# Packing the top-k of a 64-token chunk, a new order for gate copies, convolution products from PSUM, and ten products held behind the gate matrix

## The chip, the cores and the metric

The kernel runs on one core of a Trainium2 chip. The time is that of one execution on the device in microseconds (us); where several runs are given, their median counts.

## The reference

One layer of a hybrid decoder for 512 prompt tokens and 64 sample tokens (8 sequences of 8). Two branches, a gated short convolution and a sliding-window attention, are merged, and a layer norm gives h. Then comes the part that takes most of the time, a retrieval of experts by product keys: each token has 8 heads; a head has two queries of 128 numbers, each scored against 128 sub-keys; the best 16 of each side give pairs, and the best 16 pairs name 16 of the 16384 experts.

```python
qv = einsum('nd,de->ne', xb, w_pq).reshape(n, 8, 2, 128)
s = einsum('nhpc,hpkc->nhpk', qv, sub_keys)
top_s, top_i = lax.top_k(s, 16)
cand_s = top_s[:, :, 0, :, None] + top_s[:, :, 1, None, :]
best_s, sel = lax.top_k(cand_s.reshape(n, 8, -1), 16)      # idx: the experts that sel names
gate = softmax(best_s)
pre = einsum('nd,nhkd->nhk', xb, expert_u[idx])
out = einsum('nhk,nhkd->nd', gate * gelu(pre), expert_v[idx])
```

The convolution multiplies two projections, runs three taps over the product, and multiplies by a third projection.

## The kernel before, in words

The 576 tokens are cut into chunks of up to 128. A first window (chunks 0 and SMP, 256 rows) and a second window (chunks 1, 2 and 3, with 128, 128 and 64 rows) pass through the same stages: projections, attention, convolution (`conv_tile`, L378), merge, top-k (`scores`, L732, and `route`, L422). Every weight table comes through `table` (L136): a load of 512 KB on SP's queue, then `split` (L118) into a high part on ScalarE (L119) and a low part on GpSimd or VectorE (L120). A product (`mm3`, L122) is three matmuls for each of eight blocks, so 24 for one table.

The first window's experts are gathered row by row (`experts`, L491): an indirect load on GpSimd (L512), then a dot product or a scaled sum on VectorE (L526, L535). These steps are called from `table`, `PACE_U` of them for one table of `expert_u`, and so are spread over the rest of the program.

The second window's experts are computed densely. A front product (`front`, L833) multiplies all tokens by a table of `expert_u` (`euT`), applies a GELU on ScalarE (L840, L844) and, for the first `NS` = 60 tables, writes the result to a spill in DRAM. Gates are built as a matrix: for each of the 384 token columns, `gate_matrix` (L753) compares numbers with keys on VectorE (L766) to get two one-hots, scales one of them (L772 on ScalarE for three of four tokens, L774 on GpSimd for the fourth), multiplies them on TensorE (L775), and copies four tokens' 128x512 result to `gb` (L779 on ScalarE for three of four, L781 on VectorE for the fourth). A group of 16 tokens then goes to DRAM (L782); there are 24 groups.

The order is set as follows. `scores(second, g4)` is called for the quarters 0 to 3, with 5 front products after each. For a quarter, four products with `w_pq` give queries, these are multiplied by sub-keys into one PSUM bank a chunk (L742), a bank is copied to `sc` (L746), and `top16` (L414) runs five VectorE instructions for each of the 4 score sets of each chunk. After quarters 1 and 3, `route` runs for each chunk: top 16 of the sums, an exponential on ScalarE (L448), and two one-hot compares with the row `iota` (L470) that look up the key numbers. Then the gate groups are traced, with front products up to `AHEAD - KEEP` spread over them, and the last `KEEP` = 3 products are put behind the last gate matmul in TensorE's queue:

```python
    for i in range(len(DENSE)):
        for g in gate_matrix(i, *second.sel[i], gd):
            fronts(base + (AHEAD - KEEP - base) * (i * (128 // GN) + g + 1) // total)
    with tc.issue_after(newest[1]):
        fronts(AHEAD)
```

`AHEAD` is 69. The framework orders each engine's instructions by its own simulated times, so that engines work off in-order queues whose order is not exactly the traced one. PSUM has two banks for products with the tag `u` and three with the tag `mm`.

The last stage (L909) reads gates (L879) and spilled results (L883) back, multiplies them (L887), splits the product into `chi` and `clo`, and accumulates it with tables of `expert_v` into six PSUM banks (L917): 18 matmuls for a table. For tables past 60 a front product runs in between.

Of the kernel before, what the change touches and what calls it, by code (L numbers as in the profile page):

```python
# [60 lines left out]

ORDER = "qkscscasacsca"
FQ = 5
KEEP = 3
LAST = 2


# [8 lines left out]
def step_kernel(ctx: ExitStack, tc: tile.TileContext, I: dict, O: dict):  # L76
# [25 lines left out]
    def tmp(p, shape, tag, name=None, bufs=1, dt=F32):  # L102
        return pools[p].tile(shape, dt, tag=tag, name=name or tag, bufs=bufs)
# [274 lines left out]
    def conv_tile(ct, project, chi, clo, segs, smp):  # L378

        mv = chi.shape[2]  # L380
        npr = sum(b - a for a, b in segs)
        hs = tmp("t", [128, mv], "hs")
        y = hs
        up = tmp("t", [128, 2 + npr], "up")
        A.activation(hs, project(2), AF.Copy)
        cg = tmp("t", [128, mv], "cg")
        A.activation(cg, project(1), AF.Copy)
        V.tensor_copy(up[:, 0:2], ucar[:, ct, :])
        parts, at = [], 0
        for a, b in segs:  # L390
            V.tensor_tensor(up[:, 2 + at:2 + at + b - a], cg[:, a:b], hs[:, a:b], op=ALU.mult)
            parts.append((y[:, a:b], [up[:, at + j:at + j + b - a] for j in range(3)]))
            at += b - a
        V.tensor_copy(ucar[:, ct, :], up[:, npr:npr + 2])
        if smp:
            def tok(t):
                return t[:, smp:smp + 64].rearrange("p (b t) -> p b t", b=NB)

            us = tmp("t", [128, NB, 2 + NT], "us")
            V.tensor_copy(us[:, :, 0:2], state[:, ct])  # L400
            V.tensor_tensor(us[:, :, 2:], tok(cg), tok(hs), op=ALU.mult)
            V.tensor_copy(state[:, ct], us[:, :, NT:])
            parts.append((tok(y), [us[:, :, j:j + NT] for j in range(3)]))
        for dst, taps in parts:
            V.tensor_scalar(dst, taps[2], convw[:, ct, 2:3], None, op0=ALU.mult)
            V.scalar_tensor_tensor(dst, taps[0], convw[:, ct, 0:1], dst, op0=ALU.mult, op1=ALU.add)
            V.scalar_tensor_tensor(dst, taps[1], convw[:, ct, 1:2], dst, op0=ALU.mult, op1=ALU.add)
        bg = tmp("t", [128, mv], "bg")
        A.activation(bg, project(0), AF.Copy)
        V.tensor_tensor(y, y, bg, op=ALU.mult)  # L410
        split(chi[:, ct, :], clo[:, ct, :], y)


    def top16(val, pos, s, n):  # L414
        s2 = tmp("k", [128, 128], "s2", bufs=2)[:s.shape[0], :n]
        V.max(val[:, 0:8], s)
        V.max_index(pos[:, 0:8], val[:, 0:8], s)
        V.match_replace(s2, val[:, 0:8], s, -3.0e38)
        V.max(val[:, 8:16], s2)
        V.max_index(pos[:, 8:16], val[:, 8:16], s2)  # L420

    def route(val, pos, sel, hs):  # L422

        keys, gt = sel
        r = val.shape[0]
        val, pos = (t[:, hs * 8:hs * 8 + 8, :] for t in (val, pos))
        gt, keys = gt[:r, hs * 64:hs * 64 + 64], [t[:r, hs * 64:hs * 64 + 64] for t in keys]
        cand = tmp("k", [128, 4, NCAND], "cand")[:r]
        v4 = val.rearrange("p (h s) k -> p h s k", s=2)
        V.tensor_tensor(cand[:, :, 0:64].rearrange("p h (a b) -> p h a b", a=4),  # L430
                        v4[:, :, 0, 0:4].unsqueeze(3).broadcast_to([r, 4, 4, 16]),
                        v4[:, :, 1, :].unsqueeze(2).broadcast_to([r, 4, 4, 16]), op=ALU.add)
        V.tensor_tensor(cand[:, :, 64:112].rearrange("p h (a b) -> p h a b", a=12),
                        v4[:, :, 0, 4:16].unsqueeze(3).broadcast_to([r, 4, 12, 4]),
                        v4[:, :, 1, 0:4].unsqueeze(2).broadcast_to([r, 4, 12, 4]), op=ALU.add)

        def f128(tag, dt=F32):
            return tmp("k", [128, 64], tag, dt=dt)[:r]

        bv = f128("bv")  # L440
        bp = f128("bp", U32)
        for h in range(4):
            top16(bv[:, h * 16:(h + 1) * 16], bp[:, h * 16:(h + 1) * 16], cand[:, h, :], NCAND)

        b3 = bv.rearrange("p (h k) -> p h k", h=4)
        ge = f128("ge").rearrange("p (h k) -> p h k", h=4)
        V.tensor_tensor(ge, b3, b3[:, :, 0:1].broadcast_to([r, 4, 16]), op=ALU.subtract)
        A.activation(ge, ge, AF.Exp)  # L448
        gs = tmp("k", [128, 4], "gs")[:r]
        V.tensor_reduce(gs, ge, axis=AX.X, op=ALU.add)  # L450
        V.reciprocal(gs, gs)
        V.tensor_tensor(gt.rearrange("p (h k) -> p h k", h=4), ge,
                        gs.unsqueeze(2).broadcast_to([r, 4, 16]), op=ALU.mult)

        mk = f128("mk")
        V.tensor_single_scalar(mk, bp, 64, op=ALU.is_ge)
        pf = tmp("k", [128, 4, 2, 16], "pf", dt=BF16)[:r]
        V.tensor_copy(pf, pos.rearrange("p (h s) k -> p h s k", s=2))
        for k, (s1, s2, off) in enumerate((((4, ALU.logical_shift_right), (2, ALU.logical_shift_right), -12.0),
                                           ((15, ALU.bitwise_and), (3, ALU.bitwise_and), 0.0))):  # L460
            u1 = f128("u1", U32)
            u2 = f128("u2", U32)
            V.tensor_single_scalar(u1, bp, s1[0], op=s1[1])
            V.tensor_single_scalar(u2, bp, s2[0], op=s2[1])
            rk = f128("rk")
            V.scalar_tensor_tensor(rk, u2, off, u1, op0=ALU.add, op1=ALU.subtract)
            V.tensor_tensor(rk, rk, mk, op=ALU.mult)  # L467
            V.tensor_tensor(rk, rk, u1, op=ALU.add)
            oh = tmp("k", [128, 4, 16, 16], "oh", dt=BF16)[:r]
            V.tensor_tensor(oh.rearrange("p h k a -> p (h k) a"), rk.unsqueeze(2).broadcast_to([r, 64, 16]),  # L470
                            iota[:r].unsqueeze(1).broadcast_to([r, 64, 16]), op=ALU.is_equal)
            V.tensor_tensor(oh, oh, pf[:, :, k, :].unsqueeze(2).broadcast_to([r, 4, 16, 16]), op=ALU.mult)
            V.tensor_reduce(keys[k], oh.rearrange("p h k a -> p (h k) a"), axis=AX.X, op=ALU.add)

# [189 lines left out]
    def merge_attention(s):  # L664
# [59 lines left out]
        if s.w == 0:  # L724
            A.activation(h_tok[3][64:128], h_tok[SMP][64:128], AF.Copy)
        s.xs.close()
        s.val = [tmp("k", [128, 16, 16], f"val{i}")[:r] for i, r in enumerate(s.rows)]
        s.pos = [tmp("k", [128, 16, 16], f"pos{i}", dt=U32)[:r] for i, r in enumerate(s.rows)]
        s.sel = [sel3 if c == 3 else (key_tiles(), gate[c] if c in GATHER else tmp("k", [128, 128], "gt", bufs=2))
                 for c in s.chunks]  # L730

    def scores(s, g4):  # L732

        sk = tmp("w", [128, 512], "raw", name="sk", bufs=RAW["w"])
        S.dma_start(sk, I["sub_keys"][g4])
        pss = [bank("mm")[:r] for r in s.rows]
        for j in range(4):
            ps = product(s, weight(s, I["w_pq"][g4 * 4 + j]), s.hT, 8, "u")
            qv = tmp("k", [128, s.mv], "qv", bufs=2)
            A.activation(qv, ps, AF.Copy)  # L740
            for i, r in enumerate(s.rows):
                PE.matmul(pss[i][:, j * 128:(j + 1) * 128], qv[:, i * 128:i * 128 + r],  # L742
                          sk[:, j * 128:(j + 1) * 128], start=True, stop=True)
        for i in range(s.n):
            sc = tmp("kb"[s.w], [128, 4, 128], "sc", bufs=2 + s.w * 2)[:s.rows[i]]
            A.activation(sc, pss[i].rearrange("p (j n) -> p j n", j=4), AF.Copy)  # L746
            for j in range(4):
                top16(s.val[i][:, g4 * 4 + j, :], s.pos[i][:, g4 * 4 + j, :], sc[:, j, :], 128)
            if g4 % 2:
                route(s.val[i], s.pos[i], s.sel[i], g4 // 2)  # L750


    def gate_matrix(i, keys, gt, gd):  # L753
# [6 lines left out]
        for g in range(128 // GN):  # L760
            gb = tmp("b", [128, 128, GN], "gb", bufs=2)
            for q in range(GN // 4):
# [5 lines left out]
                for r in range(4):  # L768
# [4 lines left out]
                    else:  # L773
                        G.tensor_scalar(oi, oi, weight_of, None, op0=ALU.mult)  # L774
                    newest[1] = PE.matmul(ps[:, r * 128:(r + 1) * 128], hot[:, 1, r, :], oi, start=True, stop=True).ins  # L775
                dst = gb[:, :, q * 4:(q + 1) * 4].rearrange("p i n -> p n i")
                src = ps.rearrange("p (n i) -> p n i", n=4)
                if OUT[q] == "a":
                    A.activation(dst, src, AF.Copy)  # L779
                else:  # L780
# [43 lines left out]
    pools["at"] = ks.enter_context(psum("at1", 1))  # L824
    shared = [pools["at"].tile([128, 512], F32, tag="at", name="pt")]
    A.activation(shared[0][:, 384:512], iota128, AF.Copy)
    pools["hp"] = ks.enter_context(psum("hp", 1))
    pools["f"] = ctx.enter_context(pool("f", "right"))
    pools["b"] = bs.enter_context(pool("b", "right"))
# [22 lines left out]
            front(done)  # L852
            done += 1

    for g4 in range(4):
        scores(second, g4)
        fronts(FQ * (g4 + 1))
    total = len(DENSE) * 128 // GN
    base = done
    for i in range(len(DENSE)):  # L860
# [168 lines left out]
```

## Time and profile before

| | |
|---|---|
| three runs | 1908.52, 1902.17, 1897.84 us |
| median | 1902.17 us |
| the profiled execution | 1897.44 us, its span 1895.6 us |
| granted TensorE clock, mean | 0.966 of full speed |
| busy: TensorE, VectorE, ScalarE, GpSimd | 91%, 82%, 43%, 59% of the span |

The span runs from the first instruction to the last. Busy time counts an engine's own work, not its waits. PE is TensorE's matmuls, PEld its weight loads, DVE is VectorE, ACT ScalarE, POOL GpSimd, SP the queue that issues most loads. A group of instructions is given by line, engine, operation, output and inputs with their shapes, and count; then busy time and mean length of one; then the engine's idle time in front of them and what ended it.

### The profile page before, as it was taken

Reading aid. Unit: us, or ns where it says so; the run is one execution under the profiler, and the core shown is the slowest. Engines: PE = TensorE matmul, PEld = TensorE weight load, DVE = VectorE, ACT = ScalarE, POOL = GpSimd, SP = SyncE. Lnnn points to the kernel's source line nnn. Section 1 sums busy time; section 2 is a strip of 40 time slices with the busy share of each in tenths; the row PEclk is TensorE's granted clock in tenths of the full one; section 3 lists DMA queues with packets and bytes.
Section 4 is the critical chain, followed back from the end, with each engine's and each line's share of the span. In section 5 each row is a group of like instructions: output and inputs, shape, how many; then the busy total and the mean of one; then the engine's idle time right before and its main releaser. Section 6 shows DMA issues by size and latency. Waiting matters only on the chain.

```text
span 1895.6 us, 27747 instructions
## 1 busy us (share of the span) xinstructions
PE 1730.8 (91%) x9760; PEld 1566.8 (83%) x9760; DVE 1553.8 (82%) x2752; ACT 812.1 (43%) x1355; POOL 1115.9 (59%) x724
## 2 busy tenths in 40 slices
PE   8999998997979778889998789999999999999985
PEld 7897788886779778879997668877899999988974
DVE  6646679997966999999878567878778988989788
ACT  4553344433343333467888333333333333343322
POOL 4345444356766667678886212222577787777883
PEclk9999999988989898999999899999999999999998
DMA  7436443357757568679897989999999999989973
GB/s 246 151 124 217 132 136 118 112 170 258 281 205 233 205 215 286 217 263 329 331 340 288 319 273 340 337 343 344 306 329 340 323 332 348 340 311 347 317 261 110
DMA packets 190300, 496.46 MB, mean 262 GB/s; under 512 B 17472, under 2 KB 83456, under 8 KB 187072
## 3 DMA queue, kind: packets, MB, share of 16 engines
q1 hardware_dynamic: 134864, 293.34, 45.3%
q0 software_dynamic: 55296, 201.35, 30.0%
q8 instruction: 76, 1.25, 0.3%
q14 instruction: 64, 0.52, 0.1%
HBM read 454.48 MB, written 40.54 MB: 261 GB/s over the span
## 4 chain that ended last, share of the span: by engine, by line
PE 34%; DVE 27%; DMA 17%; issue 10%; POOL 7%; ACT 3%; SPq 1%; DVEq 0%; POOLq 0%; ACTq 0%
PE acc L917 10%; PE ps L124 6%; PE ps L123 6%; PE ps L125 6%; DMA g<-in_ev,idx 6%; DMA re<-spill 4%; POOL g L512 4%; POOL wlo L120 3%; PE ps L775 3%; DVE junk L526 3%; DVE wlo L120 2%; DVE h L535 2%; DMA g<-in_eu,idx 1%; ACT whi L119 1%; DVE rk L467 1%
## 5 line engine op out<-in xcount | busy, mean ns | idle before, releaser
L120 POOL TENSOR_TENSOR wlo<-raw,whi 128x1024 fp32r<-128x1024 f32 x232 | 578.0, 2493 | 306.9 <-ACT whi L119 294.0
L119 ACT ACTIVATE whi<-raw 128x1024 fp32r<-128x1024 f32 x388 | 409.0, 1055 | 519.0 <-PE ps L124 235.1
L123 PE MATMUL ps<-xhi,whi 128*128 128x384 f32 (+2 forms) x1600 | 529.7, 331 | 25.0 <-ACT sp L840 21.0
L125 PE MATMUL ps<-xhi,wlo 128*128 128x384 f32 (+2 forms) x1600 | 527.2, 330 | 0.7 <-POOL wlo L120 0.7
L124 PE MATMUL ps<-xlo,whi 128*128 128x384 f32 (+2 forms) x1600 | 527.1, 329 | 0.0
L512 POOL DMA_INDIRECT g<-in_eu,idx x192 | 206.3, 1075 | 272.0 <-DVE junk L526 218.9
L535 DVE SCALAR_TENSOR_TENSOR h<-g,pre,h 128x1024 f32<-128x1024 f32 x192 | 304.9, 1588 | 67.9 <-DMA g<-in_ev,idx 66.6
L512 POOL DMA_INDIRECT g<-in_ev,idx x192 | 259.0, 1349 | 131.1 <-DVE h L535 90.9
L123 PEld LDWEIGHTS ps<-xhi,whi 128*128 128x128 f32 x1600 | 307.4, 192 | 33.1 <-ACT sp L840 22.7
L917 PE MATMUL acc<-whi,chi 128*128 128x512 f32 x756 | 294.2, 396 | 18.4 <-ACT chi L119 18.4
L124 PEld LDWEIGHTS ps<-xlo,whi 128*128 128x128 f32 x1600 | 307.0, 192 | 4.2 <-issue 1.3
L125 PEld LDWEIGHTS ps<-xhi,wlo 128*128 128x128 f32 x1600 | 306.7, 192 | 2.4 <-POOL wlo L120 1.2
L917 PE MATMUL acc<-wlo,chi 128*128 128x512 f32 x756 | 299.9, 397 | 6.6 <-POOL wlo L120 6.6
L917 PE MATMUL acc<-whi,clo 128*128 128x512 f32 x756 | 266.2, 393 | 5.2 <-DVE clo L120 5.2
L120 DVE TENSOR_TENSOR wlo<-raw,whi 128x1024 fp32r<-128x1024 f32 x156 | 198.5, 1273 | 44.2 <-ACT whi L119 43.7
L917 PEld LDWEIGHTS acc<-whi,chi 128*128 128x128 f32 x756 | 144.3, 191 | 50.4 <-ACT chi L119 21.6
L917 PEld LDWEIGHTS acc<-wlo,chi 128*128 128x128 f32 x756 | 144.2, 191 | 38.3 <-POOL wlo L120 9.0
L917 PEld LDWEIGHTS acc<-whi,clo 128*128 128x128 f32 x756 | 142.2, 188 | 37.3 <-DVE clo L120 7.9
L526 DVE SCALAR_TENSOR_TENSOR junk<-g,hp 128x1024 bf16<-128x1024 f32 x104 | 125.5, 1206 | 45.0 <-DMA g<-in_eu,idx 43.0
L775 PE MATMUL ps<-hot 128*128 128x128 f32 x768 | 116.1, 286 | 24.8 <-ACT hot L772 21.9
L775 PEld LDWEIGHTS ps<-hot 128*128 128x128 f32 x768 | 107.9, 194 | 32.6 <-ACT hot L772 28.2
L526 DVE SCALAR_TENSOR_TENSOR junk<-g,h 128x1024 bf16<-128x1024 f32 x88 | 123.9, 1408 | 8.4 <-DMA g<-in_eu,idx 8.2
(250 smaller groups left out, 2341.8 us busy)
## 6 DMA issues: line engine op xcount, KB each, us to landing
raw<-in_euT SPq DMA_DIRECT2D x128, 512.0 KB
raw<-in_ev SPq DMA_DIRECT2D x128, 512.0 KB
gd<-gb SPq DMA_DIRECT2D x24, 1024.0 KB
gm<-gd SPq DMA_DIRECT2D x48, 512.0 KB
raw<-in_w_g SPq DMA_DIRECT2D x32, 512.0 KB
raw<-in_w_pq SPq DMA_DIRECT2D x32, 512.0 KB
raw<-in_w_bch SPq DMA_DIRECT2D x24, 512.0 KB
spill<-sp SPq DMA_DIRECT2D x60, 192.0 KB
```

What stands on the lines that cost most here:

```text
L119: A.activation(hi, src, AF.Copy)
L120: return (eng or V).tensor_tensor(lo, src, hi.bitcast(F32), op=ALU.subtract)
L123: PE.matmul(ps, L[0], R[0], start=start, stop=False)
L124: PE.matmul(ps, L[0], R[1], start=False, stop=False)
L125: PE.matmul(ps, L[1], R[0], start=False, stop=stop)
L467: V.tensor_tensor(rk, rk, mk, op=ALU.mult)
L512: G.indirect_dma_start(out=rows[i], out_offset=None, in_=I[src], in_offset=bass.IndirectOffsetOnAxis(ap=idx[c][:, s:s + 1], axis=0))
L526: V.scalar_tensor_tensor(junk, g, 1.0, in_psum(c), op0=ALU.mult, op1=ALU.mult, accum_out=p)
L535: V.scalar_tensor_tensor(h_tok[c], g, p, h_tok[c], op0=ALU.mult, op1=ALU.add)
L775: newest[1] = PE.matmul(ps[:, r * 128:(r + 1) * 128], hot[:, 1, r, :], oi, start=True, stop=True).ins
L917: PE.matmul(*args, **kw)
```

## The change

Four things change. (1) The 64-row chunk's scores for quarters 0 and 1 stay on partitions 0 to 63, those for quarters 2 and 3 go to partitions 64 to 127 of the same bank; the quarters run in the order 0, 2, 1, 3, and `top16` and `route` run once for the two halves together. The upper half's results are moved to the lower partitions by three loads. `route` in the second window reads its number row from PSUM, from the bank that the gate's transposes also write. (2) Gate copies write runs of four numbers and step through PSUM, where they read in a row and wrote with a step of 16 numbers. (3) `conv_tile` multiplies from PSUM without copying two of its three projections. (4) `KEEP` is 10.

```diff
-KEEP = 3
+KEEP = 10
@@ conv_tile
-        cg = tmp("t", [128, mv], "cg")
-        A.activation(cg, project(1), AF.Copy)
+        cg = project(1)
...
-        bg = tmp("t", [128, mv], "bg")
-        A.activation(bg, project(0), AF.Copy)
-        V.tensor_tensor(y, y, bg, op=ALU.mult)
+        V.tensor_tensor(y, y, project(0), op=ALU.mult)
@@ route
+    numbers = [iota]
...
-                            iota[:r].unsqueeze(1).broadcast_to([r, 64, 16]), op=ALU.is_equal)
+                            numbers[0][:r, :16].unsqueeze(1).broadcast_to([r, 64, 16]), op=ALU.is_equal)
@@ merge_attention
-        s.val = [tmp("k", [128, 16, 16], f"val{i}")[:r] for i, r in enumerate(s.rows)]
+        s.val = [tmp("k", [128, r // 8, 16], f"val{i}") for i, r in enumerate(s.rows)]
...
@@ scores
-        pss = [bank("mm")[:r] for r in s.rows]
+        low = g4 < 2
+        pss = []
+        for i, r in enumerate(s.rows):
+            if r == 128:
+                pss.append(bank("mm"))
+            else:
+
+                if low:
+                    s.half = bank("mm")
+                pss.append(s.half[:64] if low else s.half[64:128])
...
+                where = dict(tile_position=(0, 64)) if r == 64 and not low else {}
                 PE.matmul(pss[i][:, j * 128:(j + 1) * 128], qv[:, i * 128:i * 128 + r],
-                          sk[:, j * 128:(j + 1) * 128], start=True, stop=True)
-        for i in range(s.n):
-            sc = tmp("kb"[s.w], [128, 4, 128], "sc", bufs=2 + s.w * 2)[:s.rows[i]]
-            A.activation(sc, pss[i].rearrange("p (j n) -> p j n", j=4), AF.Copy)
+                          sk[:, j * 128:(j + 1) * 128], start=True, stop=True, **where)
+        for i, r in enumerate(s.rows):
+            if r == 64 and low:
+                continue
+            src, g = (pss[i], g4) if r == 128 else (s.half, g4 - 2)
+            sc = tmp("kb"[s.w], [128, 4, 128], "sc", bufs=2 + s.w * 2)
+            A.activation(sc, src.rearrange("p (j n) -> p j n", j=4), AF.Copy)
             for j in range(4):
-                top16(s.val[i][:, g4 * 4 + j, :], s.pos[i][:, g4 * 4 + j, :], sc[:, j, :], 128)
-            if g4 % 2:
+                top16(s.val[i][:, g * 4 + j, :], s.pos[i][:, g * 4 + j, :], sc[:, j, :], 128)
+            if r == 64 and g == 1:
+                keys, gt = s.sel[i]
+                kh, gh = [tmp("k", [128, 64], f"kh{k}") for k in range(2)], tmp("k", [128, 64], "gh")
+                route(s.val[i], s.pos[i], (kh, gh), 0)
+                for dst, src in zip((*keys, gt), (*kh, gh)):
+                    A.activation(dst[:64, :64], src[:64], AF.Copy)
+                    S.dma_start(dst[:64, 64:128], src[64:128])
+            elif r == 128 and g4 % 2:
                 route(s.val[i], s.pos[i], s.sel[i], g4 // 2)
@@ gate_matrix
-                dst = gb[:, :, q * 4:(q + 1) * 4].rearrange("p i n -> p n i")
-                src = ps.rearrange("p (n i) -> p n i", n=4)
+                dst = gb[:, :, q * 4:(q + 1) * 4]
+                src = ps.rearrange("p (n i) -> p i n", n=4)
@@ step_kernel
     A.activation(shared[0][:, 384:512], iota128, AF.Copy)
+    numbers[0] = shared[0][:, 384:512]
...
-    for g4 in range(4):
+    for k, g4 in enumerate((0, 2, 1, 3)):
         scores(second, g4)
-        fronts(FQ * (g4 + 1))
+        fronts(FQ * (k + 1))
```

## Rows read from the trace of the kernel before

**Rows 1.** Stretches: length; PE, PEld, DVE, ACT, POOL busy (instructions); clock, DMA share, GB/s.
```profile
640.00:780.00 140.00, 111.62 (x606) 108.59 (x605) 140.00 (x444) 45.95 (x65) 91.57 (x56) 0.89 0.72 238
780.00:900.00 120.00, 105.09 (x663) 100.20 (x662) 118.76 (x190) 81.96 (x166) 91.65 (x77) 1.00 0.81 277
900.00:1000.00 100.00, 99.43 (x684) 99.08 (x684) 82.32 (x99) 85.69 (x186) 83.79 (x81) 1.00 0.92 338
1000.00:1050.00 50.00, 40.63 (x266) 37.86 (x265) 39.69 (x42) 39.95 (x92) 29.54 (x33) 0.93 0.69 257
1050.00:1085.00 35.00, 26.23 (x121) 22.75 (x120) 17.75 (x24) 11.60 (x15) 9.70 (x7) 0.91 1.00 343
...
1320.00:1780.00 460.00, 456.61 (x2299) 413.59 (x2298) 394.35 (x340) 164.87 (x225) 346.47 (x210) 1.00 0.94 331
```

**Rows 2.** Waits from 570 to 1085 us: us in total, times, the longest.
```profile
ACT ge L448 <- DVE ge L447: 24.8, 5, 11.0
...
PE ps L775 <- ACT hot L772: 21.9, 22, 2.8
PE ps L123 <- ACT sp L840: 20.6, 4, 9.8
...
PE acc L917 <- ACT chi L119: 8.8, 2, 5.2
```

**Rows 3.** ScalarE's timeline: start, us, instruction, idle time before it and its releaser.
```profile
647.00 0.26 ACT L448 ACTIVATE ge<-ge 128x64 f32<-128x64 f32 x1 [11.03 <-DVE ge L447]
...
709.05 0.59 ACT L746 ACTIVATE sc<-ps 64x512 f32<-64x512 f32 x1 [12.93 <-DVE s L418]
```

**Rows 4.** TensorE's timeline from the last groups of gates to the first accumulations.
```profile
1019.75 0.28 PE L775 MATMUL ps<-hot 128*128 128x128 f32 x1
...
1048.26 0.42 PE L123 MATMUL ps<-xhi,whi 128*128 128x384 f32 x1
...
1060.67 0.34 PE L125 MATMUL ps<-xhi,wlo 128*128 128x384 f32 x1
1064.54 0.50 PE L917 MATMUL acc<-whi,chi 128*128 128x512 f32 x1 [3.54 <-ACT chi L119]
...
1083.93 0.79 PE L917 MATMUL acc<-whi,chi 128*128 128x512 f32 x1 [5.24 <-ACT chi L119]
```

**Rows 5.** Groups of ScalarE by form, whole span.
```profile
L772 ACT ACTIVATE hot<-hot,T 128x128 f32<-128x128 f32 x288 | 92.5, 392 | 54.6 <-DVE hot L766 49.4 <-issue 2.6 <-PE ps L775 1.0
L779 ACT ACTIVATE gb<-ps 128x512 f32<-128x512 f32 x72 | 74.0, 1066 | 7.5 <-PE ps L775 7.4
...
L746 ACT ACTIVATE sc<-ps 128x512 f32<-128x512 f32 x16 | 8.7, 591 | 3.4 <-PE ps L742 3.3
```

**Rows 6.** Groups of VectorE by form, whole span.
```profile
L781 DVE COPY gb<-ps 128x512 f32<-128x512 f32 x24 | 25.0, 1042 | 5.8 <-PE ps L775 5.8
...
L306 DVE COPY t<-ps 128x512 f32<-128x512 f32 x6 | 4.0, 672 | 0.1
```

**Rows 7.** Groups of VectorE by form, 566 to 880 us.
```profile
L470 DVE TENSOR_TENSOR oh<-rk,iota 128x1024 bf16<-128x1024 f32 x8 | 12.2, 1522 | 0.0
...
L470 DVE TENSOR_TENSOR oh<-rk,iota 64x1024 bf16<-64x1024 f32 x4 | 9.2, 2295 | 0.0
...
L451 DVE RECIPROCAL gs<-gs 64x4 f32<-64x4 f32 x2 | 0.3, 154 | 0.0
```

**Rows 8.** Single lines: count, ns least/median/most, first and last start in us.
```profile
L470 DVE TENSOR_TENSOR oh<-rk,iota x20: 1196/1206/3731, 300.6 to 869.5; 128x1024 bf16<-128x1024 f32 x16, 64x1024 bf16<-64x1024 f32 x4
...
L775 PE MATMUL ps<-hot x768: 270/275/582, 783.2 to 1048.2; 128*128 128x128 f32 x192
...
L782 SPq DMA_DIRECT2D gd<-gb x24: 319/320/1064, 805.6 to 1049.7; - x24
```

**Rows 9.** Groups of VectorE by form, 240 to 430 us.
```profile
L391 DVE TENSOR_TENSOR up<-cg,hs 128x320 f32<-128x320 f32 x4 | 4.0, 1010 | 0.3 <-ACT cg L387 0.3
...
L662 DVE TENSOR_TENSOR br<-cg,ps 128x320 f32<-128x320 f32 x4 | 1.9, 469 | 0.0
```

More of the change, by code (lines that the diff above doesn't have):

```diff
@@ L726, in merge_attention @@
         s.xs.close()
-        s.val = [tmp("k", [128, 16, 16], f"val{i}")[:r] for i, r in enumerate(s.rows)]
-        s.pos = [tmp("k", [128, 16, 16], f"pos{i}", dt=U32)[:r] for i, r in enumerate(s.rows)]
+        s.val = [tmp("k", [128, r // 8, 16], f"val{i}") for i, r in enumerate(s.rows)]
+        s.pos = [tmp("k", [128, r // 8, 16], f"pos{i}", dt=U32) for i, r in enumerate(s.rows)]
         s.sel = [sel3 if c == 3 else (key_tiles(), gate[c] if c in GATHER else tmp("k", [128, 128], "gt", bufs=2))
```

## The prediction

> **What bounds the kernel now.** I read the stretch table first [rows 1], because shares over the whole span mix stages with different limits. TensorE is full from 1320 to 1780 us (456.6 of 460): there nothing but less TensorE work helps, and the change takes none away. It is idle for 28.4 us of the 140 between 640 and 780, for 14.9 of the 120 to 900, for 9.4 of the 50 to 1050 and for 8.8 of the 35 to 1085. In the first of these stretches VectorE is busy for 140.0 of 140 us. So the question is how much of the 62 us of TensorE idle time between 640 and 1085 goes, because each microsecond of it is passed on to a full TensorE behind it.
>
> Then the waits of TensorE in that stretch [rows 2]: 20.6 us in four waits for ScalarE's GELU of an earlier product (it frees the product's PSUM bank), 21.9 us in 22 waits for scaled one-hots of the gate matrix, 8.8 us in two waits for coefficients of the last stage. The GELU itself is quick; the ScalarE timeline [rows 3] shows what it stood behind. At 647.0 an exponential of `route` had waited 11.0 us for VectorE, and at 709.1 a copy of scores had waited 12.9 us for VectorE to finish with an older `sc` buffer. ScalarE works in order, so TensorE stopped for 9.8 and 8.6 us behind these two. VectorE's top-k bounds 640 to 780.
>
> From 900 to 1000 TensorE is full (99.4 us). From 1019.75 [rows 4] to the last gate matmul at 1048.2 [rows 8] no product runs, only gate matmuls: 123 recorded, about four groups of 32, so 7.1 us a group. ScalarE's work on one group is twelve scalings and three copies: 12 x 0.32 + 3 x 1.03 = 6.9 us [rows 5] (busy time over count). ScalarE sets that stretch. Then come the three held products, 1048.3 to 1061.0 (4.2 us each), a wait of 3.5 us for the first coefficients, and one of 5.2 us at 1083.9 [rows 4].
>
> **Packed top-k.** For the 64-row chunk each top-16 pass and each `route` now does two sets of heads in one instruction. VectorE's instructions on 64 partitions between 566 and 880 us are 32 forms, 236 instructions, 77.1 us together; the first and the last form stand in [rows 7]. Half go: 38.5 us. The five `route` calls that are left for the second window have two one-hot compares each, and these read the number row from PSUM now. They took 1.52 us (128 rows) and 2.30 us (64 rows) on average [rows 7] against a least of 1.20 and a most of 3.73 [rows 8]; at 1.20 for all, 8 x 0.32 + 2 x 1.10 = 4.8 us go. Together 43 us of VectorE's work.
>
> How much of that TensorE sees lies between nothing (ScalarE's in-order waits move elsewhere) and all 43.3 us of its idle time from 640 to 900. I take the two long stops, 9.8 + 8.6 = 18.4 us: with the order 0, 2, 1, 3 no `route` follows the second quarter, which is where the first stop came from, and `sc` is filled ten times instead of twelve, which bears on the second. Shorter waits stay. **Term: -18.**
>
> What it adds is small. Three ScalarE copies of 64x64 and three loads of 16 KB through SP hand over the packed half: some 0.32 us each by the nearest rows (a scaling of 128 columns [rows 5], a DMA's issue [rows 8]). Their reader is the third chunk's gate matrix, behind two other chunks' gates, and if that cover failed it would be a few microseconds once. On SP they wait for VectorE's `route`; table loads queue behind them, and three raw and four split buffers cover about seven products, 29 us. The score matmuls into partitions 64 to 127 are as many as before: 0, and as a bound one gate matmul's 0.28 us for each of 8 [rows 8]. Reading the number row from the bank that the gate's transposes write makes the first transposes wait for the last `route`. Before, gates began at 783.2 while route compares started until 869.5 [rows 8]. VectorE is full either way, so this changes the order of its work, not the sum, and products run on TensorE meanwhile: 0, at most +15 (TensorE's idle time from 780 to 900, again).
>
> **Runs of four.** The 72 ScalarE copies take 1.066 us and the 24 VectorE copies 1.042 us, where plain copies of 128x512 take 0.591 and 0.672 [rows 5, 6]. No row shows a read that steps through PSUM by 512 bytes, as the new one does. Ends: no gain (reading costs what writing cost) and the plain copy. I take the plain copy, because the row that is nearest in size, engine and source, the 0.591 one, differs in layout alone. That is 72 x 0.475 = 34 us of ScalarE and 24 x 0.37 = 9 us of VectorE, but it shows only where ScalarE is the limit: a group falls from 6.9 to 5.5 us, so four groups of gates alone give 4 x 1.4 = 5.6. From 900 to 1000 TensorE was full. **Term: -6**, with ends 0 and -12 (eight such groups, if products run out earlier).
>
> The Trainium skill (SBUF — State Buffer, section "Door 1: The DMA port swizzle", its note on cachelines) says that SBUF wants at least two hits on each 16-byte line and that PSUM has 8-byte lines on which non-contiguous patterns are slow for matmuls. By it the writes become fast and each new read touches a line once, so the cost could move to the read; the sum by that would leave this term at 0. The trace agrees on the write, 1.066 against 0.591 us, and shows no such read.
>
> **Ten held products.** Seven more products, 7 x 4.2 = 29 us of TensorE, move behind the last gate matmul. Each brings along one 512 KB load on SP, a split on ScalarE and GpSimd, a GELU, and on average 1.5 expert steps (a gather on GpSimd, a dot product on VectorE). Only the matmuls are held; loads and splits may run ahead as far as the four buffers go. Behind the gates VectorE is busy for 17.8 of 35 us [rows 1], so the rest hides. Ten products take 42 us; the first coefficients were used 16.3 us after the last gate matmul (1064.5 - 1048.2), so the waits of 3.5 and 5.2 us go, and I count 2 us of later short ones: -11. Against it: TensorE loses seven products with which to fill gaps in front of the gate's end. From 900 to 1000 it was full, and there the gate simply ends earlier; where gates run alone, it does not. Bounds 0 and +29; I take +5, about half of the 9.4 us idle from 1000 to 1050, since the gate's last groups have no products then either. **Term: -6.**
>
> **Convolution.** 16 copies of PSUM to SBUF leave ScalarE, which ran beside a VectorE that was busier: 0; if that cover is gone the gain is theirs, by the plain copy at most 16 x 0.59 = 9 us [rows 5]. The products with `cg` and `bg` read PSUM; a like product with one input in PSUM took 0.469 us where the one from SBUF took 1.010 [rows 9]. For the eight products of the second window that is 8 x 0.54 = 4.3 us of VectorE. But banks are now held until VectorE gets to them, and TensorE has two `u` banks. I bound what that costs by the multiply that frees a bank and a like one in front of it, 2 x 0.47 us in each of eight tiles: 7.5. **Term: -1**, ends -9 and +7.
>
> **Sum.** -18 - 6 - 6 - 1 = -31 against the profiled execution's own 1897.4 us (its span 1895.6): 1866.4. The median of the runs shown is 1902.2, 4.8 above that execution, so on the median 1871.
>
> **Rivals.**
> (a) *The gate's end does not move.* Gates are a chain from VectorE's compare through ScalarE's scaling to the matmul and the copy. If that chain sets the end and TensorE does not, the seven products taken from in front leave a hole, and ten then cost 42 us behind it. The point that decides: the last gate matmul must come before 1064.5 + 5.2 + 2 - 42 = 1030 us of the span (the first use of coefficients, the later waits that go, ten products), else the kernel is slower. If it comes at 1045, it is 15 us slower: 1917. For: 28 us of gates alone at the end already, and 21.9 us of waits for scalings. Against: from 900 to 1000 TensorE was full, and both ScalarE and VectorE lose work. Chance 0.12.
> (b) *The copy does not get faster* (the change does not do what it says): the strided read costs what the strided write did. Term two is 0: 1877. If ScalarE's gates then also hold the end by 4 us, 1881. Still faster. Chance 0.20. That would be the rule of SBUF — State Buffer, cited from the Trainium skill above.
> (c) *The stops move.* The exponentials and copies still stand in ScalarE's order behind VectorE, now after the third and fourth quarters, and PSUM banks held by the convolution cost 5 of their 7.5 us. Then -18 becomes 0 and -1 becomes +5: 1895. For: ScalarE's exponentials waited 24.8 us for VectorE in five places [rows 2]. Against: VectorE has 43 us less to do. Chance 0.15.
> The forecast itself has 0.53.
>
> **How the numbers follow.** About 0.5% (9.5 us) is what a measurement of this kernel can tell from no change. Forecast and (b) are faster: 0.73. (c) is within 0.5%: 0.15. (a) is slower: 0.12. The forecast's own ends are the bounds of its terms: with twice the packing term and the far end of the copies, 1871 - 18 - 6 = 1847, so I put the low end at 1846; with half of packing lost and +7 in the convolution, 1871 + 9 + 8 = 1888. To hold (b) and (c) the range goes up to 1900; (a) and a little below 1846 are left out.
>
> **What would show it.** Right: VectorE's top-16 forms on 64 rows gone and its time in 566 to 880 about 43 us less; the waits of TensorE for the GELU well under 20.6 us; the gate copies near 0.59 and 0.67 us; the last gate matmul at about 1000 us (1030 less the sum's 30), 985 to 1015; no wait in front of the first two coefficients; the last stage as long as before and shifted by some 30 us. Wrong: a last gate matmul after 1030, gate copies still above 1 us, or new waits of TensorE for VectorE between 240 and 430 us, where the convolution holds banks.

## The result, and the profile after

The changed kernel takes 1878.5 us (median of four runs, 1874.3 to 1883.3) where the kernel before takes 1900.0 (four runs): a ratio of 0.9886, 95% interval 0.9846 to 0.9927, about 21.6 us faster. The forecast was 31 us. Sign and range held, and the sum came near for partly wrong reasons: two terms were too small, one too large, and one had the wrong sign. The profiled execution of after took 1882.1 us, its span 1880.3.

The stretch table of after, read against [rows 1] (columns as there):

```profile
640.00:780.00 140.00, 119.35 (x655) 116.32 (x654) 138.39 (x438) 50.67 (x68) 90.03 (x56) 0.91 0.75 249
780.00:900.00 120.00, 113.01 (x727) 112.66 (x726) 105.18 (x152) 76.44 (x173) 103.02 (x88) 0.96 0.92 328
900.00:1000.00 100.00, 86.23 (x584) 80.44 (x583) 87.95 (x96) 82.77 (x227) 57.39 (x72) 0.97 0.65 249
1000.00:1050.00 50.00, 44.60 (x252) 43.33 (x251) 21.68 (x23) 21.44 (x43) 27.78 (x21) 0.93 0.87 305
1050.00:1085.00 35.00, 29.63 (x130) 25.24 (x129) 27.20 (x35) 9.99 (x14) 16.62 (x12) 0.90 0.94 327
```

Up to 900 TensorE does 15.7 us more than before (7.7 and 7.9 in the first two rows). From 900 to 1000, where it was full (99.4), it now does 13.2 less: a hole has opened in front of the gate's end. The same stretch cut where products run out, from the last product ahead of the gate's end to the last gate matmul, before and then after:

```profile
1016.90:1048.50 31.60, 22.23 (x140) 19.46 (x139) 24.22 (x25) 26.58 (x64) 15.45 (x21) 0.89 0.64 244
```
```profile
931.20:1008.90 77.70, 62.51 (x423) 55.77 (x422) 69.78 (x74) 68.01 (x195) 34.63 (x53) 0.96 0.53 210
```

Gates run alone for 77.7 us instead of 31.6. Some 416 gate matmuls lie in it, 13 groups of 32 at 6.0 us, where before it was 138, 4.3 groups at 7.3 us. ScalarE is busy for 68.0 of it and VectorE for 69.8, so both engines of the gate's chain are busy for nearly nine tenths of it, and TensorE, busy for 62.5, waits for them. The gate matmuls and the copies of the whole kernel (count; minimum, median and maximum in ns; first and last start):

```profile
L794 PE MATMUL ps<-hot x768: 270/275/582, 813.5 to 1008.4; 128*128 128x128 f32 x192
```
```profile
L798 ACT ACTIVATE gb<-ps x72: 574/597/602, 816.8 to 1007.8; 128x512 f32<-128x512 f32 x72
```
```profile
L800 DVE COPY gb<-ps x24: 678/685/692, 823.3 to 1008.7; 128x512 f32<-128x512 f32 x24
```

The copies cost what plain ones cost [rows 5, 6], 0.60 and 0.69 us, and the last gate matmul starts at 1008.4, 39.8 us earlier than before [rows 8]. But the first accumulation comes only 2.2 us earlier (TensorE's timeline; [rows 4] for before):

```profile
1041.80 0.69 PE L123 MATMUL ps<-xhi,whi 128*128 128x384 f32 x1 [3.98 <-ACT gel L864]
...
1062.36 0.77 PE L937 MATMUL acc<-whi,chi 128*128 128x512 f32 x1 [5.37 <-ACT whi L119]
```

From the gate's end to the first accumulation it is now 54.0 us instead of 16.3. The rest of the gain lies behind: from the first accumulation to the end of the span it is 817.9 us instead of 831.1, because the wait of 5.24 us at 1083.9 [rows 4] and shorter ones are gone.

TensorE's waits from 570 to 900 have changed their kind. Before (the two classes that matter, cut to this stretch):

```profile
PE ps L775 <- ACT hot L772: 13.0, 10, 2.8
PE pt L756 <- DVE kk L473: 7.5, 2, 5.1
```

After:

```profile
PE ps L123 <- ACT sp L860: 27.4, 7, 10.1
PE ps L125 <- POOL wlo L120: 1.0, 1, 1.0
```

All its waits there fell from 44.0 to 28.4 us, but the waits behind the GELU, the ones I meant to remove, grew from 20.6 to 27.4. ScalarE's exponentials still stand behind VectorE, and two new stops follow them (ScalarE, then TensorE):

```profile
758.05 0.26 ACT L447 ACTIVATE ge<-ge 128x64 f32<-128x64 f32 x1 [11.58 <-DVE ge L446]
...
793.05 0.26 ACT L447 ACTIVATE ge<-ge 128x64 f32<-128x64 f32 x1 [9.60 <-DVE ge L446]
```
```profile
761.11 0.69 PE L123 MATMUL ps<-xhi,whi 128*128 128x384 f32 x1 [10.08 <-ACT sp L860]
...
796.11 0.69 PE L123 MATMUL ps<-xhi,whi 128*128 128x384 f32 x1 [6.99 <-ACT sp L860]
```

### The profile page after: what moved, and what is told of

Its sections match the earlier page's. It is cut to its first block, busy times and chain, and to the rows that moved or that the text cites. A ratio compares the mean times of both kernels' runs of the same rounds, so it can differ in the third digit from the quotient of the medians.

```text
span 1880.3 us, 27617 instructions
## 1 busy us (share of the span) xinstructions
PE 1733.5 (92%) x9760; PEld 1573.5 (84%) x9760; DVE 1507.2 (80%) x2632; ACT 782.1 (42%) x1339; POOL 1111.2 (59%) x724
## 4 chain that ended last, share of the span: by engine, by line
PE 49%; DVE 24%; DMA 10%; issue 7%; POOL 5%; ACT 5%; SPq 1%; DVEq 0%; POOLq 0%; ACTq 0%
PE acc L937 19%; PE ps L123 9%; PE ps L124 8%; PE ps L125 8%; POOL wlo L120 3%; DMA re<-spill 3%; DVE junk L525 3%; PE ps L794 2%; POOL g L511 2%; DVE wlo L120 2%; DMA raw<-in_euT 2%; ACT whi L119 1%; ACT hot L791 1%; DMA g<-in_eu,idx 1%; DVE s L415 1%
## 5 line engine op out<-in xcount | busy, mean ns | idle before, releaser
L534 DVE SCALAR_TENSOR_TENSOR h<-g,pre,h 128x1024 f32<-128x1024 f32 x192 | 316.2, 1647 | 71.7 <-DMA g<-in_ev,idx 70.4
L511 POOL DMA_INDIRECT g<-in_ev,idx x192 | 255.0, 1328 | 126.5 <-DVE h L534 87.3
L937 PE MATMUL acc<-whi,clo 128*128 128x512 f32 x756 | 258.1, 394 | 2.1 <-DVE clo L120 2.1
L120 DVE TENSOR_TENSOR wlo<-raw,whi 128x1024 fp32r<-128x1024 f32 x156 | 204.6, 1312 | 49.1 <-ACT whi L119 48.9
L785 DVE TENSOR_TENSOR hot<-pt,T 128x1024 f32<-128x1024 f32 x96 | 114.0, 1217 | 17.1 <-PE ps L794 12.1
L794 PE MATMUL ps<-hot 128*128 128x128 f32 x768 | 111.6, 289 | 15.2 <-ACT hot L791 14.0
```

The source lines that it names most:

```text
L120: return (eng or V).tensor_tensor(lo, src, hi.bitcast(F32), op=ALU.subtract)
L511: G.indirect_dma_start(out=rows[i], out_offset=None, in_=I[src], in_offset=bass.IndirectOffsetOnAxis(ap=idx[c][:, s:s + 1], axis=0))
L534: V.scalar_tensor_tensor(h_tok[c], g, p, h_tok[c], op0=ALU.mult, op1=ALU.add)
L785: V.tensor_tensor(hot, iota_ps.unsqueeze(1).unsqueeze(1).broadcast_to([128, 2, 4, 128]), T[:, 0:2, n:n + 4].unsqueeze(3).broadcast_to([128 ...
L937: PE.matmul(*args, **kw)
```

## The experiments

My theory after the result: the gate's end came early because seven products left its front and because packing and copies took load off VectorE and ScalarE; the held products then gave it back behind the gate. The rival was the prediction's own account, held products worth 6 us. Each kernel was timed beside the kernel before. "Before" was 1899.2, 1896.5 and 1898.0 us in the three groups of four (e1 to e4, e5 to e8, e9 to e12), so kernels are compared by their ratios, and 0.001 is 1.9 us. The interval of after itself is 0.004 to either side, so a difference from after of under about 8 us is not settled by the times alone. Line numbers move by a few between kernels.

### Held products: e1, e2, e7

e1 is before with ten, e2 after with three (shown), e7 after with five:

```diff
-KEEP = 10
+KEEP = 3
```

> The kernel before with ten held products instead of three and nothing else. As predicted (the held products alone are worth 6 us): 1894 us, no wait in front of the first two coefficients, last gate matmul at about 1022 (1048 less some 26). Rival, held products give back what they take: the gate's chain (VectorE compare, ScalarE scaling and copy at 7.1 us a group) ends at 1028 or later because it runs alone for longer, ten products then take 42 us and the table of the second expert matrix still comes late: first accumulation at 1072 to 1080 instead of 1064.5, 1900 to 1908 us.

> The changed kernel with three held products again. As predicted (held products are worth 6 us): 1884.5 us, 6 slower than the changed kernel's 1878.5. Rival, held products give back what they take: the seven products fill the gate-only stretch of 966 to 1008 us, the last gate matmul comes at 1015 to 1030 instead of 1008.7, three products (12.7 us) and some 8 us of waits for coefficients and table follow, first accumulation at 1040 to 1052 instead of 1062.4, 1865 to 1877 us even with 6 us of later waits back.

> The changed kernel with five held products. With ten the last gate matmul came at 1008.7 and with three at 1029.6, 3.0 us earlier for each held product that costs 4.2 behind it; with three, TensorE still waited 3.2, 6.2 and 1.6 us for coefficients of the last stage. If two more products cover the wait of 6.2 and part of the 3.2: 2 x 1.2 lost and 6 to 9 gained, 1865 to 1869 us. If those waits end with the loads, which start only once the gate matrix is written and so move with its end: 1870 to 1875 us, between three and ten.

Measured: e1 1904.4 us, ratio 1.0024 (1.0006 to 1.0042), so ten held products alone make the old kernel slower. e2 1872.1 us, 0.9849 (0.9822 to 0.9876), and its five runs (1865.3 to 1874.7) lie below or beside the lowest of after's four. e7 1863.0 us, 0.9820 (0.9782 to 0.9859), six runs from 1857.9 to 1870.0, all below after's lowest. The last gate matmuls of e1, e2 and e7:

```profile
L775 PE MATMUL ps<-hot x768: 270/275/580, 782.4 to 1032.8; 128*128 128x128 f32 x192
```
```profile
L794 PE MATMUL ps<-hot x768: 270/275/582, 815.8 to 1029.3; 128*128 128x128 f32 x192
```
```profile
L794 PE MATMUL ps<-hot x768: 270/275/422, 811.3 to 1017.5; 128*128 128x128 f32 x192
```

and the stops behind them, e1, e2, e7:

```profile
1067.27 0.69 PE L123 MATMUL ps<-xhi,whi 128*128 128x384 f32 x1 [5.09 <-ACT gel L844]
...
1087.74 0.77 PE L917 MATMUL acc<-whi,chi 128*128 128x512 f32 x1 [5.34 <-issue]
```
```profile
1045.30 0.50 PE L937 MATMUL acc<-whi,chi 128*128 128x512 f32 x1 [3.22 <-ACT chi L119]
...
1065.64 0.79 PE L937 MATMUL acc<-whi,chi 128*128 128x512 f32 x1 [6.19 <-ACT chi L119]
```
```profile
1039.53 0.63 PE L937 MATMUL acc<-whi,chi 128*128 128x512 f32 x1 [5.10 <-ACT chi L119]
1058.06 0.50 PE L937 MATMUL acc<-whi,chi 128*128 128x512 f32 x1 [0.21 <-ACT chi L119]
```

The balance of seven more held products, worked out from these spans. From e2 to after: the gate ends 20.9 us earlier (1029.3 to 1008.4), the way to the first accumulation is 38.0 longer (16.0 to 54.0), the rest 8.2 shorter (826.1 to 817.9): 8.9 us lost, which is the difference of the spans (the ratios say 7). From before to e1: 15.4 earlier, 38.6 longer, 13.8 shorter: 9.4 lost (the ratio says 4.6: these are single executions). So of seven products' 29 us the gate's end gives back 15 to 21, since gates alone go no faster than ScalarE and VectorE let them, and up to the first accumulation 38 us are paid and not 29. With five the wait of 6.2 is down to 0.2 and no stop falls among the products, though the wait in front of the first accumulation is 5.1 where three products left 3.2. The first case of the expectation, 1865 to 1869 us, was near, even a little high.

### The stop among the ten: e8

```diff
-        A.activation(hi, src, AF.Copy)
+        if top is None:
+            A.activation(hi, src, AF.Copy)
+        else:
+            top.tensor_copy(hi, src)
...
-                   PACE_V[t >= NS])
+                   PACE_V[t >= NS], V if t < 3 else None)
```

> The changed kernel with the rounded copies of the first three tables of the second expert matrix made by VectorE, not ScalarE; ten held products stay. If the stop of 4.0 us among the held products and the lowered clock behind it come from ScalarE waiting in order for such a table ahead of a GELU: the stop goes, the ten products take 42 to 44 us instead of 48.3, 1871 to 1875 us. If the loads themselves are what comes late: the stop goes but the wait in front of the first accumulation grows by as much, first accumulation still at 1060 to 1064, 1877 to 1880 us.

Measured: 1877.3 us, 0.9888 (0.9848 to 0.9928), no difference from after. The wait of 5.37 in front of the first accumulation went (it came at 1058.1), but the stop stayed. The time is that of the second case, whose course was not seen either. TensorE and ScalarE of e8:

```profile
1042.24 0.69 PE L126 MATMUL ps<-xhi,whi 128*128 128x384 f32 x1 [4.40 <-ACT gel L867]
```
```profile
1039.47 1.06 ACT L120 ACTIVATE whi<-raw 128x1024 fp32r<-128x1024 f32 x1 [9.43 <-DMA raw<-in_ev]
```

The edit took the wrong tables away from ScalarE. It still waited 9.4 us for a table of the second expert matrix, though the first three are no longer its work. GpSimd waited beside it; in after:

```profile
1040.06 7.35 POOL L120 TENSOR_TENSOR wlo<-raw,whi 128x1024 fp32r<-128x1024 f32 x3 [8.78 <-DMA raw<-in_ev]
```

The kernel gives GpSimd the low part of a table of this matrix only from table 60 on (60 to 124). Such tables have split buffers of their own (`v`), two of them, which are free at this point, so tables 60 and 61 are loaded and split early. When the two are split, GpSimd finishes the held products' tables, and its next split, which needs table 60's buffer again, starts only at 1332.1. The chain that ended last (start, us, what) shows how these loads reach TensorE in after:

```profile
1021.90 6.71 SPq L899
1028.65 1.68 SPq L138
1030.38 9.91 DMA raw<-in_ev
1040.31 1.06 ACT whi L119
1041.36 0.39 ACT gel L864
1041.80 0.69 PE ps L123
```

A load of gates (L899) holds SP's queue for 6.7 us, the table's load behind it lands at 1040.3, ScalarE copies the table, and only then comes the GELU that frees the bank, of a product that TensorE had finished some 7 us before. ScalarE waits in the same way in e1 (10.1 us for such a table, until 1064.5). So the mechanism that I had in mind, ScalarE waiting in its order for such a table ahead of a GELU, fits both traces, but for two tables that are wanted some 290 us later and not for the first three. It is read from the traces and not shown by a run: none moved these two tables.

### The gate copy alone: e3

```diff
-                dst = gb[:, :, q * 4:(q + 1) * 4]
-                src = ps.rearrange("p (n i) -> p i n", n=4)
+                dst = gb[:, :, q * 4:(q + 1) * 4].rearrange("p i n -> p n i")
+                src = ps.rearrange("p (n i) -> p n i", n=4)
```

> The changed kernel with the old gate copy (plain read of PSUM, writes that step by 64 bytes). As predicted: gate copies back at 1.06 us on ScalarE and 1.04 on VectorE, 6 us slower, 1884.5 us. Rival, ten held products make the gate-only stretch longer (eight groups from 966 to 1008 us at 5.33 us each): eight groups at 6.9 us end 12.6 us later, last gate matmul at about 1021, 1889 to 1892 us. If the read cost what the write did: same copy times, 0.

Measured: 1888.6 us, 0.9945 (0.9926 to 0.9964), 11.2 us slower than after by the ratios. The copies are back at 1.05 us. The gates-only stretch of e3:

```profile
933.70:1021.30 87.60, 64.91 (x423) 58.93 (x422) 73.66 (x74) 80.27 (x195) 34.49 (x53) 0.90 0.47 187
```

It starts within 3 us of after's and holds the same 13 groups; they take 9.9 us longer (87.6 against 77.7), with ScalarE busy for 80.3. A group of 16 tokens thus gained 0.76 us by the new copy. The rival's time is met, its eight groups are not: I had read the stretch from 966 on, and products had run out at 931.

### Packing and the number row: e4, e6, e9

e4 is after with the packing undone, that is with one bank for each chunk's scores and `top16` and `route` on 64 partitions as before:

```diff
-                pss.append(s.half[:64] if low else s.half[64:128])
+        pss = [bank("mm")[:r] for r in s.rows]
...
-    for k, g4 in enumerate((0, 2, 1, 3)):
+    for k, g4 in enumerate((0, 1, 2, 3)):
```

e6 is after with the number row in SBUF, and e9 has both edits:

```diff
-    numbers[0] = shared[0][:, 384:512]
```

> The changed kernel with the 64-row chunk unpacked again (order of quarters 0, 1, 2, 3); the number row stays in PSUM. As predicted (18 us, nearly all from packing): 1896 us, stops of TensorE of 8 us and more behind ScalarE's exponential and score copy back between 640 and 780. Rival, the stops only moved and VectorE's relief is taken up in the gate-only stretch: 1879 to 1886 us, last gate matmul within 6 us of 1008.7.

> The changed kernel with the number row of the one-hot compare read from SBUF again, so that the gate's transposes no longer wait for the last route. As predicted (the row in PSUM saves 4.8 us of VectorE's work, part of the packing term): one to three us slower, 1880 to 1882 us; compares of 128 rows back at 1.5 us. Rival, the wait of the transposes for the last route costs more than that: gates start near 785 instead of 813, last gate matmul before 1004, 1870 to 1876 us. Third case, VectorE's work is conserved and the order of gates and route does not matter: within 1.5 us of 1878.5.

> The changed kernel with the 64-row chunk unpacked and the number row in SBUF again: the whole of what the prediction called the packing term is undone. As predicted: 18 us slower, 1896 us. If packing (13.5 by the run that undid it alone) and the row in PSUM (a loss of 7 by its run) simply add: 6 to 7 us slower than the changed kernel, 1883 to 1886. If the row's wait costs only where packing is there: 1891 to 1894.

Measured: e4 1893.5 us, 0.9957 (0.9937 to 0.9977), 13.5 slower than after; e6 1867.9, 0.9851 (0.9815 to 0.9887), 6.6 faster; e9 1889.1, 0.9947 (0.9927 to 0.9968), 11.6 slower. e4 lies between its two cases: TensorE's waits behind the GELU from 570 to 900 grow from 27.4 to 36.9 us, and the last gate matmul is 15 us later than in after and not within 6; e6 is its rival in time and in the gate's end (1002.3); e9 is nearer to its third case than to the sum of the other two. The whole term that the prediction put at 18 is thus about 12. The four kernels also give each part beside either state of the other: packing is worth 13.5 us with the row in PSUM (e4 to after) and 18.2 with the row in SBUF (e9 to e6); the row in PSUM costs 1.9 us without packing (e9 to e4) and 6.6 with it (e6 to after), both within the intervals. In e9 the two stretches from 640 to 900 read:

```profile
640.00:780.00 140.00, 111.52 (x604) 108.49 (x603) 140.00 (x446) 45.95 (x65) 89.68 (x56) 0.89 0.73 235
780.00:900.00 120.00, 106.24 (x673) 101.94 (x672) 117.84 (x190) 71.73 (x166) 93.34 (x78) 1.00 0.82 281
```

as before, and after does 14.6 us more TensorE work in them. That is packing's gain at its place; the gates-only stretch behind passes on most of it. The row is another matter. TensorE's waits from 570 to 900 in e6:

```profile
PE ps L123 <- ACT sp L859: 14.9, 5, 4.9
PE pt L775 <- DVE kk L472: 7.2, 1, 7.2
PE ps L794 <- ACT hot L791: 6.5, 6, 1.9
```

28.6 us in sum, where after has 28.4: with the row in SBUF the transposes start at 743.7 and not at 806.2, the gates' waits are back, and the waits behind the GELU fall by as much. The row changes which waits there are and not how long they are together. VectorE is not relieved by it either: the ten compares and the multiplies behind them take 30.5 us between 566 and 880 in after and 30.0 in e6.

So packing's own effect on the waits is read from e9 to e6, where the row is in SBUF in both. The two largest classes of e9, of 42.5 us in sum:

```profile
PE ps L123 <- ACT sp L839: 19.9, 4, 9.8
PE ps L774 <- ACT hot L771: 11.8, 10, 2.8
```

Packing takes away 13.9 us of TensorE's waits: 5.0 behind the GELU, whose longest stop falls from 9.8 to 4.9, and most of the rest in front of gate matmuls.

### The convolution: e5, e10

e5 is after with the old copies (shown), e10 before with the new products:

```diff
-        cg = project(1)
+        cg = tmp("t", [128, mv], "cg")
+        A.activation(cg, project(1), AF.Copy)
```

(e5; the same for `bg`; e10 is the opposite edit.)

> The changed kernel with the convolution's two products copied to SBUF by ScalarE again. As predicted (the edit is worth 1 us): 1879 to 1880 us. Rival, banks held until VectorE gets to them cost more than VectorE's shorter products give: 1871 to 1875 us, and TensorE's waits for attention's exponential, 16.4 us between 240 and 430, back towards the 4.6 of before. Other rival, VectorE has so much less to do in 240 to 430 that the edit is worth more: 1883 us or above.

> The kernel before with the convolution's products reading PSUM and nothing else. As predicted: 1 us faster, 1896 to 1899 us beside 1897 to 1900 of before. If the 5 to 6 us that undoing it cost in the changed kernel belong to the convolution itself, TensorE's first GELU of the expert products comes at least 4 us earlier than 559.2, 1891 to 1895 us. If they come from how the later work falls into place: first GELU within 2.5 us of 559.2, and the time within 3 us of before.

Measured: e5 1882.6 us, 0.9918 (0.9894 to 0.9941), 6.1 slower than after; e10 1891.5, 0.9966 (0.9945 to 0.9988), 6.5 faster than before. Both say 6, from either side, beyond what the prediction gave; e10's time lies in its second case, its first GELU between the second and the third. The first GELU comes at 556.5 in e10 and at 559.2 in before; at 560.0 in e5 and at 557.5 in after: 2.5 to 2.7 us of it are the convolution's own. VectorE's two products, in after:

```profile
L390 DVE TENSOR_TENSOR up<-ps,hs 128x320 f32<-128x320 f32 x4 | 1.9, 471 | 0.0
L407 DVE TENSOR_TENSOR hs<-hs,ps 128x320 f32<-128x320 f32 x4 | 1.9, 471 | 0.0
```

They fell from 1.01 and 0.94 to 0.47 us. But VectorE as a whole was not relieved: from 240 to 570 it was busy for 286.1 us in before, 294.8 in e10 and 292.6 in after. Neighbours of the two products became longer; the first tap's product, a one-input product from SBUF to SBUF, went from 374 to 928 ns in after and to 926 in e10. So the gain cannot be put down to VectorE's shorter products. In e10's one profile it is 2.7 us at the first GELU, 3.3 at the gate's end and 7.8 at the end of the span, so most of it shows only in the last stage. Why, no run here settles.

### Putting the findings together: e11, e12

After with the row in SBUF and five (e11) or six (e12) held products:

> The changed kernel with five held products and the number row in SBUF. If the two findings are independent (15 us for five held products, 7 for the row): 1855 to 1858 us, the best of all; last gate matmul at 1007 to 1013, first accumulation at 1029 to 1036. If both remove the same idle time of TensorE ahead of the gate's end: 1861 to 1865 us, no better than five held products alone.

> As the run with five, with six held products. If the loads of the last stage still set its first accumulation, a sixth product costs only what it leaves idle ahead of the gate's end: within 2 us of the run with five. If the wait is covered at five: 1 to 3 us slower than five.

Measured: e11 1871.7 us, 0.9852 (0.9825 to 0.9878); e12 1865.9, 0.9823 (0.9802 to 0.9844). Both missed: the gains do not add, and with five the row in PSUM is the better one (last gate matmul 1017.5 there, 1021.3 in e11). With ten it was the worse one (1008.4 against 1002.3). Since the waits ahead of 900 are the same in sum, I take the row for neutral, with a few microseconds either way by how the gates fall between products; that is an interpretation, since the runs show no cause for the sign. The best kernels are e7 and e12, 32 to 34 us faster than before and some 12 faster than after; their intervals overlap.

## Why the prediction was right, and where it was wrong

By its own terms, with what undoing each one cost (signs as in the sum):

- **Packed top-k, -18: measured -12 together with the number row, -13.5 or -18.2 alone.** The size was right with the row in SBUF. Of the step "the two long stops go", what failed is the changed kernel as a whole: stops of 10.1 and 7.0 us replaced 9.8 and 8.6, and ScalarE's exponentials waited 35.3 us in five waits where before they waited 24.8, as rival (c) had it. In e6, with the row in SBUF, no wait behind the GELU is longer than 4.9 us, and e4, unpacked with the row in PSUM, has 36.9 us of such waits where e9 has 19.9; so the new stops come with the row and not with packing. Packing also shortened the waits in front of gate matmuls (13.6 us in e9, 6.5 in e6), which I had said would stay. VectorE's relief is near the forecast of 43 us: its busy time over the span is 1507.2 us in after and 1555.1 in e9, which undoes packing and row alone, 47.9 less. From 566 to 880 alone, where the prediction looked for it, it fell by only 31.4 us against before, perhaps since other work moved in.
- **Number row, 0 at most +15: measured +2 to +7, not clear of the intervals.** The compare fell to 1.21 us as forecast, but the multiply behind it rose from 1.16 to 1.84 us, so the 4.8 us counted for it did not come. The first transposes did come 49 us later, for no change in the sum of TensorE's waits.
- **Runs of four, -6: measured -11.** The price per copy was right to 0.02 us and rival (b) is out, and with it the page of the Trainium skill cited there, as far as it was carried over to these engines' reads. The count was wrong: 13 groups ran alone and not four, and each gained 0.76 us and not 1.4, so that 4 x 1.4 = 5.6 became 13 x 0.76 = 9.9: two errors that partly cancel. ScalarE was busy for 80.3 of 87.6 us with the old copy and for 68.0 of 77.7 with the new one, and VectorE is busy for 69.8 of the latter, which suggests that ScalarE no longer sets that stretch alone. I took the number of groups from the kernel before, while two other parts of the change, fewer products in front and a faster VectorE, make that stretch longer.
- **Ten held products, -6: measured +5 (on before) to +7 (on after).** This is the step that failed. "Against it +5" should have been 8.5 to 14, the part of 29 us that the gate's end does not give back: rival (a) had the mechanism, and e1 shows it at 1032.8, past the 1030 where it was to decide. And "-11 for waits" was only half true: 8 to 14 us of later waits went, but 8.6 to 9.2 came in among and behind the held products (in after a stop of 4.0, the wait of 5.4 where three products left 3.2, the rest a lowered clock). I had costed the loads as running ahead "as far as the four buffers go", and not the order of the engines: ScalarE took two tables of the last stage's second half in between, whose loads stood on SP behind the gates' loads, and a held product's GELU waited behind them.
- **Convolution, -1: measured -6**, inside its ends of -9 and +7. The two products did become shorter (8 x 0.5 against the 4.3 us forecast), but VectorE's other work took more than that back. No new wait of TensorE for VectorE above 2.3 us appeared between 240 and 430 us, but the one for attention's exponential rose from 4.6 to 16.4 us (16.5 in e10), and the stretch to the first GELU still got 2.5 shorter. So the term was mis-sized, and its cause is open.

-12 - 11 + 7 - 6 = -22 against 21.6 measured: the undoings add up, closer than their intervals promise, so that part is luck. That the forecast held its range is in part luck too: the two terms that were too small, 10 us together, cover most of the 13 by which held products missed. Of what would show it, the last gate matmul (1008.4, forecast 985 to 1015) and the copies came right; "VectorE about 43 us less from 566 to 880", "GELU waits well under 20.6", "no wait in front of the first two coefficients" and "the last stage as long as before" did not.

## What to carry to other kernels

Work that is held back to cover a later wait costs its whole length behind the point, and gives back in front of it only what the chain there can do faster. So count how much earlier the point itself moves (here 2 to 3 us for each product of 4.2), and hold only as much as the wait needs: of three, five and ten, five was best here. Look, too, at what engines that work in order will take up between the held pieces. And when several parts of a change meet at one stretch, read that stretch's length as the others leave it, not as it was before, or each term has the wrong count.

## What the runs showed of the hardware

A read of PSUM that steps by 512 bytes cost ScalarE and VectorE nothing that can be seen: 0.597 and 0.685 us for 128x512, where the plain copies of [rows 5, 6] took 0.591 and 0.672, while single floats written 64 bytes apart in SBUF cost 1.05 and 1.03 (e3). The Trainium skill (SBUF — State Buffer, section "Door 1: The DMA port swizzle") speaks of slow non-contiguous PSUM patterns for matmuls; for these two engines' copies no run here shows any.

The clock was low right behind the stop among the held products: after the 3.98 us of idle time that end at 1041.80 the granted clock of 1042.3 to 1046.7 was 0.50, and matmuls of 128x384 that otherwise started 0.17 us apart were 0.32 apart until 1047:

```profile
1042.28 0.53 PE L124 MATMUL ps<-xlo,whi 128*128 128x384 f32 x1
1042.60 0.53 PE L125 MATMUL ps<-xhi,wlo 128*128 128x384 f32 x1
```

That is the lower of TensorE's two levels (1.2 against 2.4 GHz), and the 4.8 us from 1042.28 on did what takes 2.6 at the other spacing: 2.2 us, the rest of the balance of held products.
